# FFN in of a hybrid decoder block: splits one piece earlier, a weight sum moved from an adding DMA to VectorE, first sums by DMA, the second norm in a written order

## The chip, the cores and the metric

The kernel runs on 1 core of one Trainium2 chip. The metric is the device time of one launch, in microseconds; the profile adds the span of one profiled execution on that core. PE is TensorE, DVE VectorE, ACT ScalarE, POOL GpSimd and SP SyncE, which only issues DMAs here.

## What is computed

One layer, 512 tokens by 1024 features, all in float32:

```
mod = silu(c) @ mod_w + mod_b                 # shift1 scale1 gate1 shift2 scale2 gate2
h = rms_norm(x, g_pre_mix) * (1 + scale1) + shift1
...                                           # three mixers on h @ w_in, merged
mix_out = merged @ w_o
x = x + gate1 * rms_norm(mix_out, g_post_mix)
h2 = rms_norm(x, g_pre_ffn) * (1 + scale2) + shift2
gt, up = split(h2 @ w_ffn_in, 2)              # 1024 x 5632
f = (silu(gt) * up) @ w_ffn_out               # 2816 x 1024
x = x + gate2 * rms_norm(f, g_post_ffn)
```

The change lies between `mix_out` and `f`.

## The kernel before

**Products in three parts.** Every float32 operand of a matmul is split in two (`split`, L154 and L155): ACT casts it to a rounded copy (`whi`), DVE takes the difference to it (`wlo`). A product is then three matmuls (`mm3`): hi by hi, hi by lo, lo by hi. A weight piece is 128x1024; ACT's cast and DVE's difference of a later piece are issued when an earlier one is used: `piece()` splits up to `LOOK` = 3 pieces, the current one among them. Four buffers each hold `whi` and `wlo`.

**FFN in by seven products.** The 22 column blocks of 128 in each of gate and up are taken as 11 units of two (`u` = 0 to 10). A unit's 2x2 block product (two halves of the features by two column blocks, for two halves of the tokens) is done with seven products in place of eight. Its weights arrive as two raw tiles, `un[0]` and `un[1]`, each with two halves of the features. Four of the seven pieces are halves as loaded: q1, q2 from `un[0]`, q4 and q7 from `un[1]`, where q7's half has `un[0]`'s first half added to it. The other three are made in one tile, `wsum`, by running sums: q5 is the sum of the two halves of `un[1]` (DVE, L266); an adding DMA from POOL's queue (L274) then adds a half of `un[0]` for q6, and a second one the other half for q3. The half for q7 is added by another DMA of POOL (L267). A DMA of this kind reads its destination, adds, and writes. The second adding DMA of a unit can go only after q6's `wlo`, which reads the tile.

**A unit's steps.** From unit 2 on the pieces are used in the order 5, 1, 4, 6, 7, 2, 3; each is a `step` (L1135) of 24 matmuls of 256 columns. q5, q4, q7 and q1 each have a bank of PSUM of their own. After step 7, `gated_m1` builds two of the four output blocks `c` with three DVE operations (L1159, L1160, L1162) and takes their sigmoid on ACT (`sigm`, L164 to L166, three activations); its products on DVE (L1144, L1145) are held back until after the next piece's split (`flush`). Step 2 adds into q1's bank and gives a third block (`gated_m0`); step 3 adds into q5's bank, once c has read it, and `third_of` (L1167) gives the fourth. Units 0 and 1 are run together, product by product, since the token halves become ready late.

**What sets the order.** In FFN in, PE, DVE and ACT run in the order in which the code is written (`manual_schedule`). Each engine takes its own queue in order, and an instruction whose input isn't there holds up all behind it. SP loads raw tiles when their buffers come free, about a unit ahead.

**The second norm.** Between `w_o` and FFN in, each block of 128 tokens goes through `x1_chain`: squares of the two PSUM halves (ACT, L1048), `rstd_from` (Ln and Exp on ACT, L150, L151), the scaled product by `G1` (DVE, L1055), the add into `x1` (L1057), squares of that, its product by the second scale on POOL (`xm`, L1060), a second `rstd_from`, and the last scale and shift on DVE (L1065). `h2_tr` (L1074) transposes the result; `t1r` to `t4r` are the sums of token halves that the seven products need, each two DVE operations from `hbh` and `hbl` and a split.

**FFN out.** Its first operand, `fparts`, is the split of a finished unit; unit 0's is made in the last unit, ahead of step 3, the others one after another as the products need them.

Of the kernel before, what the change touches and what calls it, by code (L numbers as in the profile page):

```python
# [7 lines left out]
F32 = mybir.dt.float32  # L8
# [5 lines left out]
P = 128  # L14
# [18 lines left out]
def hybrid_block(ctx: ExitStack, tc, x, c, mod_w, mod_b, g_pre_mix, g_post_mix, g_pre_ffn,  # L33
# [35 lines left out]
    def q2(name, dt=F32):  # L69
        return tq.tile([P, 512], dt, tag="q2", name=name, bufs=12)  # L70
# [3 lines left out]
    def t2(name, dt=F32):  # L74
        return tp.tile([P, 512], dt, tag="t2", name=name, bufs=NT2)
# [92 lines left out]


    chunks, pieces, raws = [], [], []  # L170
    at = {"dma": 0, "split": 0, "use": 0, "raw": 0}

    def w_cols(src, c0, n=256):

# [69 lines left out]
    def wino_load(u, i):  # L244
# [6 lines left out]
        for g in range(2):  # L251
# [3 lines left out]
        units[u][i] = [raw[:, :, 4 * a:4 * a + 4].rearrange("p g k n -> p g (k n)")  # L255
                       for a in range(2)]

    def wino_piece(u, q):
        if u not in units:
            units[u] = {}  # L260
            for i in range(1 if u == 1 else 2):
                wino_load(u, i)
        un = units[u]
        if q == 5:
            un["s"] = late_pool["fx"].tile([P, 2, 512], F32, tag="wsum", name="wsum", bufs=2)
            vec.tensor_tensor(un["s"], un[1][0], un[1][1], ALU.add)  # L266
            nc.gpsimd.dma_start(un[1][0], un[0][0], accum_op=ALU.add)  # L267
        src = {1: (0, 0), 2: (0, 1), 4: (1, 1), 7: (1, 0)}.get(q)
        src = un[src[0]][src[1]] if src else un["s"]
        hi = wp.tile([P, 1024], FR, tag="whi", name="whi").rearrange("p (g n) -> p g n", g=2)  # L270
        lo = wp.tile([P, 1024], FR, tag="wlo", name="wlo").rearrange("p (g n) -> p g n", g=2)
        split(hi, lo, src)
        if q in (5, 6):
            nc.gpsimd.dma_start(un["s"], un[0][q - 5], accum_op=ALU.add)  # L274
        return [t_.rearrange("p g (k n) -> p g k n", k=4) for t_ in (hi, lo)]
# [768 lines left out]
    def x1_chain(tb, pos):  # L1044
        st = sm.tile([P, 6], F32, tag="st", name="st", bufs=4)
        for hf in range(2):
            sq = t2("sq2")
            act.activation(sq, pos[hf], AF.Square, accum_out=st[:, hf:hf + 1])  # L1048
        vec.tensor_tensor(st[:, 0:1], st[:, 0:1], st[:, 1:2], ALU.add)
        rstd_from(st[:, 2:3], st[:, 0:1], D)  # L1050
        xms = []
        for hf in range(2):
            t_ = t2("t2k")
            xv = x1[:, tb, half(hf)]
            vec.scalar_tensor_tensor(t_, pos[hf], st[:, 2:3], G1[hf], op0=ALU.mult,  # L1055
                                     op1=ALU.mult)
            vec.tensor_tensor(xv, xv, t_, ALU.add)  # L1057
            act.activation(t_, xv, AF.Square, accum_out=st[:, 3 + hf:4 + hf])
            xm = q2("xm")
            pool.tensor_tensor(xm, xv, SC[hf], ALU.mult)  # L1060
            xms.append(xm)
        vec.tensor_tensor(st[:, 3:4], st[:, 3:4], st[:, 4:5], ALU.add)
        rstd_from(st[:, 5:6], st[:, 3:4], D)
        for hf in range(2):
            vec.scalar_tensor_tensor(xms[hf], xms[hf], st[:, 5:6], SH[hf], op0=ALU.mult,  # L1065
                                     op1=ALU.add)
        return xms

    def h2_tr(tb, xms):
        pts = []  # L1070
        for q in range(2):
            pt = bank("pt2")
            for j in range(4):
                pe.transpose(pt[:, blk(j)], xms[q][:, blk(j)], ident)  # L1074
            pts.append(pt.rearrange("p (k t) -> p k t", k=4))
        return pts

    def h2_tiles(tb, xms):

        for q, p3 in enumerate(h2_tr(tb, xms)):  # L1080
            split(hbh[:, q, :, blk(tb)], hbl[:, q, :, blk(tb)], p3)

    todo = []
    for tp2 in range(2):
        tbs = (2 * tp2, 2 * tp2 + 1)
        pos = {tb: [bank("pwo") for _ in range(2)] for tb in tbs}
        ws = {}
        for k in range(KD - LATE):
            ws[k] = piece()
            for tb in tbs:  # L1090
                wo_mm(pos[tb], tb, ws[k], k)
            if todo and k >= 2:
                h2_tiles(*todo.pop(0))
        for k in range(KD - LATE, KD):
            ws[k] = piece()
        for tb in tbs:
            for k in range(KD - LATE, KD):
                wo_mm(pos[tb], tb, ws[k], k)
            todo.append((tb, x1_chain(tb, pos[tb])))


    ma.close()
    fp = ctx.enter_context(tc.tile_pool(name="fp", bufs=1, reuse_waits="tile"))
    fxs = ExitStack()
    fx = fxs.enter_context(tc.tile_pool(name="fx", bufs=1, reuse_waits="tile"))
    late_pool.update(fp=fp, fx=fx)
    wino_load(1, 1)

    def f4_tile(name, dt=F32):
        return fp.tile([P, 2, T], dt, tag="f4", name=name, bufs=NU)  # L1110
# [61 lines left out]
        fhs.append(parts_[0])  # L1172
        fls.append(parts_[1])
    f4s, fhs, fls, pts = [], [], [], {}
    with tc.manual_schedule(engines={ET.PE, ET.DVE, ET.Activation}):
# [6 lines left out]
        for u in range(2):  # L1182
            fresh(1)
            act.copy(u2s[u], pb_[1][u])
        for u in range(2):
            step(2, pb_[1][u], False, True)
            pts[u] = h2_tr(*todo.pop(0))

        t1_, b22, t2_, t3_, t4_ = (f4_tile(n) for n in ("t1r", "b22", "t2r", "t3r", "t4r"))

        def k4(t_, u):
            return t_[:, u, :].rearrange("p (k t) -> p k t", k=4)

        def parts_of(q, t_, u):
# [4 lines left out]
        for q in (6, 7, 4):  # L1199
            tx[q] = [[q2("tx", FR).rearrange("p (k t) -> p k t", k=2) for _ in range(2)]  # L1200
                     for _ in range(2)]
        tks = [slice(u * P, (u + 1) * P) for u in range(2)]
        for u in range(2):
# [4 lines left out]
            act.copy(k4(b22, u), pts[u][1])  # L1208
        for u in range(2):
# [6 lines left out]
            flush()  # L1216
        fresh(5)
        fresh(5)
        for u in range(2):
            vec.tensor_tensor(k4(t3_, u), k4(b22, u), pts[u][0], ALU.subtract)  # L1220
            parts_of(7, t3_, u)
# [1 line left out]
            fresh(6)  # L1223
            vec.tensor_tensor(u2s[u], pb_[6][u], u2s[u], ALU.add)
        for u in range(2):
            vec.tensor_tensor(k4(t4_, u), hbh[:, 1, :, tks[u]].bitcast(F32), k4(t2_, u), ALU.add)
            vec.tensor_tensor(k4(t4_, u), k4(t4_, u), hbl[:, 1, :, tks[u]].bitcast(F32), ALU.add)
# [10 lines left out]
        for u in range(2, NU):  # L1238
            f4s.append(f4_tile("f4"))
            p5 = bank("pf5")  # L1240
            step(5, p5, True, True)
            p1, u2 = bank("pf1"), temp("u2", 512, 2)
            step(1, p1, True, True)
            act.copy(u2, p1)
            p4 = bank("pf4")
            step(4, p4, True, True)
            p6 = bank("pf6")
            step(6, p6, True, True)
            vec.tensor_tensor(u2, p6, u2, ALU.add)
# [10 lines left out]
        flush()  # L1260
    fxs.close()
    tqs.close()
    fo = ctx.enter_context(tc.tile_pool(name="fo", bufs=1, reuse_waits="tile"))
# [100 lines left out]
```

## Time and profile before

| | |
|---|---|
| median of 3 runs | 868.24 us (867.53 to 868.84) |
| profiled execution, its own time | 870.63 us |
| its span | 868.9 us |
| mean granted clock of PE | 0.975 |
| PE, DVE, ACT, POOL busy | 90%, 64%, 49%, 20% of the span |
| end of w_o, transition, units 2 to 10 of FFN in, FFN out | to 431.4, to 499.7, to 731.0, to 868.9 us |
| adding DMAs wsum<-wraw | 22 of 512 KB, median 6.0 us from issue to landing |
| adding DMAs wraw<-wraw | 11 of 512 KB, median 5.2 us |

A row of the page's groups names a line, an engine, an operation, and output<-input by the program's names, then how often, its busy time and the idle time ahead of it with what ended most of that. A row of the timeline has the start, the length and, in brackets, how long the engine stood idle and what released it. A row of the windows has from:to, the length, then busy time and count of PE, PE's weight loads, DVE, ACT and POOL, PE's clock, the share of the DMA engines and GB/s. A row of the waits has a total, how often, and the longest.

### The profile page before, as it was taken

The numbers are of one execution on the slowest core, as the hardware profiler recorded it, in microseconds if no ns is written. First come the engines' busy times: TensorE is split into PE (matmuls) and PEld (weight loads), VectorE is DVE, ScalarE is ACT, GpSimd is POOL, SyncE is SP. The second block draws the span as 40 slices with busy tenths as digits, with TensorE's granted clock in tenths as the row PEclk, the third lists the DMA queues.
The fourth block names the chain that finished last, engine by engine and source line by source line (L and its number), as shares of the span: only waits on it lengthen the run. The fifth ranks groups of instructions, "written<-read, shape, count | busy, mean of one in ns | idle before, by whom it ended". The sixth has DMA issues, their size and how long they took to land. (4 is left out here: it accounts for less than half of the span.)

```text
span 868.9 us, 11371 instructions
## 1 busy us (share of the span) xinstructions
PE 779.5 (90%) x4357; PEld 664.8 (77%) x4357; DVE 558.7 (64%) x801; ACT 421.6 (49%) x703; POOL 173.0 (20%) x208
## 2 busy tenths in 40 slices
PE   4899999999999999999859688788888888899997
PEld 3679887776788888878758677788788787678886
DVE  5999876678475665367777657556565676853223
ACT  5557544766673645336535444544445455523112
POOL 4344323355211110122241011111111110000000
PEclk9999999999999999999988999999999999999999
DMA  9963422114257867375356556687676647351302
GB/s 281 296 202 97 129 68 95 49 57 153 82 185 211 264 188 233 108 221 201 109 108 131 150 106 137 147 170 158 139 153 132 125 105 228 106 212 62 114 1 97
DMA packets 122390, 126.14 MB, mean 145 GB/s; under 512 B 4124, under 2 KB 93264, under 8 KB 122336
## 3 DMA queue, kind: packets, MB, share of 16 engines
q1 hardware_dynamic: 109008, 99.62, 37.3%
q0 software_dynamic: 12560, 24.73, 16.0%
q10 hardware_dynamic: 768, 1.07, 0.3%
q8 instruction: 34, 0.56, 0.3%
q14 instruction: 20, 0.16, 0.1%
HBM read 102.33 MB, written 2.10 MB: 120 GB/s over the span
## 5 line engine op out<-in xcount | busy, mean ns | idle before, releaser
L155 DVE TENSOR_TENSOR wlo<-wraw,whi 128x1024 fp32r<-128x1024 f32 (+1 forms) x133 | 164.1, 1243 | 106.3 <-ACT whi L154 106.2
L154 ACT CAST whi<-wraw 128x1024 fp32r<-128x1024 f32 (+1 forms) x133 | 135.5, 1032 | 123.1 <-PE pgt L159 33.6
L1135 PE MATMUL pf<-hbh,whi 128*128 128x256 f32 x352 | 102.9, 292 | 28.7 <-DVE c L1160 11.8
L1135 PE MATMUL pf<-tx,whi 128*128 128x256 f32 x528 | 101.0, 293 | 8.9 <-ACT whi L154 8.9
L1135 PE MATMUL pf<-hbh,wlo 128*128 128x256 f32 x352 | 101.7, 289 | 7.4 <-DVE wlo L155 7.4
L1135 PE MATMUL pf<-hbl,whi 128*128 128x256 f32 x352 | 100.9, 287 | 0.1
L1135 PEld LDWEIGHTS pf<-hbh,whi 128*128 128x128 f32 x352 | 68.6, 195 | 32.6 <-issue 13.3
L1135 PEld LDWEIGHTS pf<-tx,whi 128*128 128x128 f32 x528 | 84.8, 197 | 10.8 <-ACT whi L154 10.7
L1135 PE MATMUL pf<-tx,wlo 128*128 128x256 f32 x264 | 77.6, 294 | 8.0 <-DVE wlo L155 7.9
L1135 PEld LDWEIGHTS pf<-hbh,wlo 128*128 128x128 f32 x352 | 68.8, 195 | 9.5 <-DVE wlo L155 9.5
L158 PE MATMUL pgt<-hh,whi 128*128 128x512 f32 x192 | 75.6, 394 | 0.0
L160 PE MATMUL pgt<-hh,wlo 128*128 128x512 f32 x192 | 75.4, 393 | 0.0
L159 PE MATMUL pgt<-hl,whi 128*128 128x512 f32 x192 | 75.0, 391 | 0.0
L155 DVE TENSOR_TENSOR wlo<-wsum,whi 128x1024 fp32r<-128x1024 f32 x33 | 40.3, 1223 | 50.3 <-ACT whi L154 50.2
L1135 PEld LDWEIGHTS pf<-hbl,whi 128*128 128x128 f32 x352 | 68.9, 196 | 0.5 <-DVE hbl L155 0.4
L158 PE MATMUL pfo<-whi,fparts 128*128 128x512 f32 x154 | 62.3, 405 | 5.5 <-ACT fparts L154 5.5
L154 ACT CAST whi<-wsum 128x1024 fp32r<-128x1024 f32 x33 | 34.2, 1040 | 66.7 <-DMA wsum<-wraw 61.0
L160 PE MATMUL pfo<-whi,fparts 128*128 128x512 f32 x154 | 61.9, 406 | 0.3 <-DVE fparts L155 0.3
L159 PE MATMUL pfo<-wlo,fparts 128*128 128x512 f32 x154 | 61.8, 401 | 0.0
L1135 PEld LDWEIGHTS pf<-tx,wlo 128*128 128x128 f32 x264 | 52.3, 198 | 10.5 <-DVE wlo L155 10.5
L274 POOL DMA_DIRECT2D wsum<-wraw x22 | 26.4, 1204 | 109.2 <-DVE wlo L155 109.2
L974 DVE SCALAR_TENSOR_TENSOR macc<-wraw,sc,macc 128x512 f32<-128x512 f32 x56 | 42.6, 761 | 7.7 <-ACT macc L972 4.7
(385 smaller groups left out, 1709.7 us busy)
## 6 DMA issues: line engine op xcount, KB each, us to landing
wraw<-in_w_ffn_in_dram SPq DMA_DIRECT2D x44, 512.0 KB, 6.7
wraw<-in_w_in_dram SPq DMA_DIRECT2D x20, 1024.0 KB, 5.2
wraw<-in_mod_w_dram SPq DMA_DIRECT2D x16, 1024.0 KB, 5.9
wsum<-wraw POOLq DMA_DIRECT2D x22, 512.0 KB, 6.0
wraw<-in_w_ffn_out_dram SPq DMA_DIRECT2D x10, 1024.0 KB, 5.0
wraw<-in_mod_w_dram SPq DMA_DIRECT2D x16, 512.0 KB, 6.8
wraw<-in_w_o_dram SPq DMA_DIRECT2D x8, 1024.0 KB, 5.2
wraw<-wraw POOLq DMA_DIRECT2D x11, 512.0 KB, 5.2
```

The lines of the kernel that those rows point to most:

```text
L154: act.copy(hi, src)
L155: vec.tensor_tensor(lo, src, hi.bitcast(F32), ALU.subtract)
L158: pe.matmul(o, whi, xhi, start=start, stop=False)
L159: pe.matmul(o, whi, xlo, start=False, stop=False)
L160: pe.matmul(o, wlo, xhi, start=False, stop=stop)
L274: nc.gpsimd.dma_start(un["s"], un[0][q - 5], accum_op=ALU.add)
L974: vec.scalar_tensor_tensor(acc, mw[:, r], c_, acc, op0=ALU.mult, op1=ALU.add)
L1135: pe.matmul(o[:, cs], a_[:, g, k, :], b_, start=(start and g + k + part == 0), stop=(stop and k == 3 and part == 2), skip_group_check=True)
```

## The change

- From the second half of `w_o` on, `piece()` splits up to 4 pieces, not 3 (for one step of the transition again 3).
- For units 2 to 10 the half for q7 is added on DVE (L284), when q4 is split, in place of POOL's DMA.
- For units 0 and 1, q5's sum is made by DMA: SP loads half of `un[1]` a second time straight into `wsum` (four loads of 256 KB, L267), and POOL's adding DMAs add the other half (L271). Their q7 halves stay with POOL's DMA (L272).
- `x1_chain` becomes five functions. The product by `G1` is made in PSUM beside the rstd; one DVE operation then scales and adds into `x1`; `xm` is made on DVE, not POOL. For blocks 2 and 3 the functions are called in a written order with the last matmuls of `w_o`, inside the manual schedule.
- ACT copies the transposes as they are (`braw`, 4 of them), and `t1r` and `t4r` take one DVE operation each from the copy in place of two.
- `fparts` of unit 0 is made after the last unit's step 5.

```diff
-        while at["split"] < min(i + LOOK, n_pieces):
+        while at["split"] < min(i + at["look"], n_pieces):
...
+    def wino_open():
+
+        for u in range(2):
+            units[u]["s"] = wsum_tile()
+            for g in range(2):
+                c0 = g * FFN + (2 * u + 1) * P
+                nc.sync.dma_start(units[u]["s"][:, g].rearrange("p (k n) -> p k n", k=4),
+                                  w_ffn_in[0:512, c0:c0 + P].rearrange("(k p) n -> p k n", k=4))
+            if u:
+                wino_load(1, 1)
+            nc.gpsimd.dma_start(units[u]["s"], units[u][1][1], accum_op=ALU.add)
+            nc.gpsimd.dma_start(units[u][1][0], units[u][0][0], accum_op=ALU.add)
...
-        if q == 5:
-            un["s"] = late_pool["fx"].tile([P, 2, 512], F32, tag="wsum", name="wsum", bufs=2)
+        if q == 5 and u > 1:
+            un["s"] = wsum_tile()
             vec.tensor_tensor(un["s"], un[1][0], un[1][1], ALU.add)
-            nc.gpsimd.dma_start(un[1][0], un[0][0], accum_op=ALU.add)
+        if q == 4 and u > 1:
+            vec.tensor_tensor(un[1][0], un[1][0], un[0][0], ALU.add)
...
+    def chain_norm(tb, pos):
+
+        st = sts[tb]
         vec.tensor_tensor(st[:, 0:1], st[:, 0:1], st[:, 1:2], ALU.add)
         rstd_from(st[:, 2:3], st[:, 0:1], D)
         for hf in range(2):
+            vec.tensor_tensor(pos[hf], pos[hf], G1[hf], ALU.mult)
+
+    def chain_x1(tb, pos, junk):
+        st, xms[tb] = sts[tb], []
+        xvs = [x1[:, tb, half(hf)] for hf in range(2)]
+        for hf, xv in enumerate(xvs):
+            vec.scalar_tensor_tensor(xv, pos[hf], st[:, 2:3], xv, op0=ALU.mult, op1=ALU.add)
+            act.activation(junk(), xv, AF.Square, accum_out=st[:, 3 + hf:4 + hf])
+        for hf, xv in enumerate(xvs):
+            xms[tb].append(q2("xm"))
+            vec.tensor_tensor(xms[tb][hf], xv, SC[hf], ALU.mult)
...
+            raws2[q, tb] = q2("braw").rearrange("p (k t) -> p k t", k=4)
+            act.copy(raws2[q, tb], p3)
...
+        if tp2:
+            at["look"] = 4
...
+        late_mm(2)
+        chain_sq(2, pos[2])
+        chain_norm(2, pos[2])
+        late_mm(3)
+        chain_x1(2, pos[2], lambda: t2("sq2"))
+        chain_sq(3, pos[3])
+        chain_norm2(2)
+        chain_norm(3, pos[3])
+        chain_h2(2)
...
+        wino_open()
...
-            vec.tensor_tensor(k4(t1_, u), hbh[:, 0, :, tks[u]].bitcast(F32), pts[u][0],
-                              ALU.subtract)
-            vec.tensor_tensor(k4(t1_, u), k4(t1_, u), hbl[:, 0, :, tks[u]].bitcast(F32), ALU.add)
+            vec.tensor_tensor(k4(t1_, u), raws2[0, u], pts[u][0], ALU.subtract)
...
             step(5, p5, True, True)
+            if u == NU - 1:
+                t_ = fp.tile([P, 2, 2, T], FR, tag="raw4", name="fparts", bufs=1)
+                f_parts(0, (t_[:, 0], t_[:, 1]))
...
-            if u == NU - 1:
-                t_ = fp.tile([P, 2, 2, T], FR, tag="raw4", name="fparts", bufs=1)
-                f_parts(0, (t_[:, 0], t_[:, 1]))
```

How this moves the queues shows best in the order of the instructions. DVE in one of the units 2 to 10, before, from the splits of q7 and q2 (`wlo<-wraw x2`) to the fourth block's `u`; the first `wlo<-wsum` is q3's, the second the next unit's q5:

```order
L155 TENSOR_TENSOR wlo<-wraw,whi 128x1024 x2
L1249 TENSOR_TENSOR u_4861<-pf_4921,u_4861 128x512
L155 TENSOR_TENSOR wlo<-wsum,whi 128x1024
L1159 TENSOR_TENSOR c_4980<-pf_4951,u_4861 128x512
L1160 SCALAR_TENSOR_TENSOR c_4980<-pf_4829,c_4980 128x512
L1162 TENSOR_TENSOR c_4980<-pf_4892,c_4980 128x512
L266 TENSOR_TENSOR wsum<-wraw 128x1024
L155 TENSOR_TENSOR wlo<-wsum,whi 128x1024
```

And now the same stretch:

```order
L155 TENSOR_TENSOR wlo<-wraw,whi 128x1024 x2
L155 TENSOR_TENSOR wlo<-wsum,whi 128x1024
L1316 TENSOR_TENSOR u_4874<-pf_4933,u_4874 128x512
L282 TENSOR_TENSOR wsum<-wraw 128x1024
L155 TENSOR_TENSOR wlo<-wsum,whi 128x1024
L1195 TENSOR_TENSOR c_5001<-pf_4963,u_4874 128x512
L1196 SCALAR_TENSOR_TENSOR c_5001<-pf_4841,c_5001 128x512
L1198 TENSOR_TENSOR c_5001<-pf_4904,c_5001 128x512
```

The sum and the split for the next unit's q5 have moved from behind the three operations of c to ahead of them, and the add into `u` from ahead of q3's split to behind it.

DVE further on in the same unit, before; `wlo<-wraw` is here q1's and then q4's of the next unit, the last row q6's, and `f<-sg,u` begins the products of the fourth block:

```order
L1145 TENSOR_TENSOR f_4828<-f_4828,c_4980 128x512
L155 TENSOR_TENSOR wlo<-wraw,whi 128x1024
L1144 TENSOR_TENSOR f_4828<-sg_5028,pf_4860 128x256
L1145 TENSOR_TENSOR f_4828<-f_4828,pf_4860 128x256
L1167 TENSOR_TENSOR u_4861<-pf_4829,u_4861 128x512
L155 TENSOR_TENSOR wlo<-wraw,whi 128x1024
L1144 TENSOR_TENSOR f_4828<-sg_5063,u_4861 128x256
L1145 TENSOR_TENSOR f_4828<-f_4828,u_4861 128x256
L155 TENSOR_TENSOR wlo<-wsum,whi 128x1024
```

And now, from the end of c's products to the fourth block's:

```order
L1181 TENSOR_TENSOR f_4840<-f_4840,c_5001 128x512
L284 TENSOR_TENSOR wraw<-wraw 128x2x512
L155 TENSOR_TENSOR wlo<-wraw,whi 128x1024
L1180 TENSOR_TENSOR f_4840<-sg_5039,pf_4873 128x256
L1181 TENSOR_TENSOR f_4840<-f_4840,pf_4873 128x256
L1203 TENSOR_TENSOR u_4874<-pf_4841,u_4874 128x512
L155 TENSOR_TENSOR wlo<-wsum,whi 128x1024
L1180 TENSOR_TENSOR f_4840<-sg_5075,u_4874 128x256
L1181 TENSOR_TENSOR f_4840<-f_4840,u_4874 128x256
```

The new add stands ahead of q4's split; q6's split now follows the add into `u` directly, with q4's split and the fourth block's products no longer between.

ACT in the transition now: `st` and `sg_3833` belong to the norm of the last block, the two casts of `wsum` are q5's of units 0 and 1, and the copies of `u` are what PE's steps 2 of units 0 and 1 wait for:

```order
L154 CAST whi<-wraw 128x1024
L1236 COPY u_3800<-pf_3802 128x512
L1081 ACTIVATE sg_3833,st<-x_3361 128x512
L1081 ACTIVATE sg_3836,st<-x_3361 128x512
L154 CAST whi<-wsum 128x1024
L1239 COPY u_3801<-pf_3842 128x512
L150 ACTIVATE st<-st,eps_c 128x1
```

Before, both copies of `u` stood ahead of both casts; the first cast now stands ahead of the second copy.

More of the change, by code (lines that the diff above doesn't have):

```diff
@@ L170, in hybrid_block @@
     chunks, pieces, raws = [], [], []
-    at = {"dma": 0, "split": 0, "use": 0, "raw": 0}
+    at = {"dma": 0, "split": 0, "use": 0, "raw": 0, "look": LOOK}
     def w_cols(src, c0, n=256):
@@ L256, in wino_load, with wsum_tile @@
                        for a in range(2)]
+    def wsum_tile():
+        return late_pool["fx"].tile([P, 2, 512], F32, tag="wsum", name="wsum", bufs=2)
+    def wino_open():
[9 more added lines that the diff above has]
+            nc.gpsimd.dma_start(units[u][1][0], units[u][0][0], accum_op=ALU.add)
     def wino_piece(u, q):
@@ L1042, in wo_mm, with chain_sq, chain_norm2, chain_h2 @@
                 w[1][:, 0, half(hf)], k == 0, k == KD - 1)
[L1044 to L1045 removed]
+    sts, xms = {}, {}
+    def chain_sq(tb, pos):
+        st = sts[tb] = sm.tile([P, 6], F32, tag="st", name="st", bufs=4)
         for hf in range(2):
[L1047 to L1048 removed]
+            act.activation(t2("sq2"), pos[hf], AF.Square, accum_out=st[:, hf:hf + 1])
+    def chain_norm(tb, pos):
+        st = sts[tb]
         vec.tensor_tensor(st[:, 0:1], st[:, 0:1], st[:, 1:2], ALU.add)
         rstd_from(st[:, 2:3], st[:, 0:1], D)
[L1051 removed]
         for hf in range(2):
[L1053 to L1061, printed above, removed]
+            vec.tensor_tensor(pos[hf], pos[hf], G1[hf], ALU.mult)
[8 more added lines that the diff above has]
+            vec.tensor_tensor(xms[tb][hf], xv, SC[hf], ALU.mult)
+    def chain_norm2(tb):
+        st = sts[tb]
         vec.tensor_tensor(st[:, 3:4], st[:, 3:4], st[:, 4:5], ALU.add)
         rstd_from(st[:, 5:6], st[:, 3:4], D)
+    def chain_h2(tb):
         for hf in range(2):
[L1065 to L1069, printed above, removed]
+            vec.scalar_tensor_tensor(xms[tb][hf], xms[tb][hf], sts[tb][:, 5:6], SH[hf],
+                                     op0=ALU.mult, op1=ALU.add)
+    def h2_tr(tb):
         pts = []
@@ L1073, in h2_tr, with h2_tiles, late_mm @@
             for j in range(4):
-                pe.transpose(pt[:, blk(j)], xms[q][:, blk(j)], ident)
+                pe.transpose(pt[:, blk(j)], xms[tb][q][:, blk(j)], ident)
             pts.append(pt.rearrange("p (k t) -> p k t", k=4))
         return pts
-    def h2_tiles(tb, xms):
-        for q, p3 in enumerate(h2_tr(tb, xms)):
+    raws2 = {}
+    def h2_tiles(tb):
+        for q, p3 in enumerate(h2_tr(tb)):
             split(hbh[:, q, :, blk(tb)], hbl[:, q, :, blk(tb)], p3)
+            raws2[q, tb] = q2("braw").rearrange("p (k t) -> p k t", k=4)
+            act.copy(raws2[q, tb], p3)
+    def late_mm(tb):
+        for k in range(KD - LATE, KD):
+            wo_mm(pos[tb], tb, ws[k], k)
     todo = []
@@ L1092, in hybrid_block @@
             if todo and k >= 2:
-                h2_tiles(*todo.pop(0))
+                h2_tiles(todo.pop(0))
         for k in range(KD - LATE, KD):
             ws[k] = piece()
+        if tp2:
+            break
         for tb in tbs:
[L1097 to L1107, printed above, removed]
+            late_mm(tb)
+            chain_sq(tb, pos[tb])
+            chain_norm(tb, pos[tb])
+            chain_x1(tb, pos[tb], lambda: t2("sq2"))
+            chain_norm2(tb)
+            chain_h2(tb)
+            todo.append(tb)
     def f4_tile(name, dt=F32):
@@ L1174, in hybrid_block @@
     f4s, fhs, fls, pts = [], [], [], {}
-    with tc.manual_schedule(engines={ET.PE, ET.DVE, ET.Activation}):
+    rest = ctx.enter_context(ExitStack())
+    rest.enter_context(tc.manual_schedule(engines={ET.PE, ET.DVE, ET.Activation}))
+    if True:
+        late_mm(2)
[7 more added lines that the diff above has]
+        chain_h2(2)
+        ma.close()
+        fp = ctx.enter_context(tc.tile_pool(name="fp", bufs=1, reuse_waits="tile"))
+        fxs = ExitStack()
+        fx = fxs.enter_context(tc.tile_pool(name="fx", bufs=1, reuse_waits="tile"))
+        late_pool.update(fp=fp, fx=fx)
+        wino_open()
         pb_ = {1: [], 5: [], 6: [], 7: [], 4: []}
@@ L1181, in hybrid_block @@
         u2s = [temp("u2", 512, 2) for _ in range(2)]
[L1182 to L1187, printed above, removed]
+        fresh(1)
+        act.copy(u2s[0], pb_[1][0])
+        chain_x1(3, pos[3], lambda: temp("sg1", 512))
+        fresh(1)
+        act.copy(u2s[1], pb_[1][1])
+        chain_norm2(3)
+        step(2, pb_[1][0], False, True)
+        pts[0] = h2_tr(2)
         t1_, b22, t2_, t3_, t4_ = (f4_tile(n) for n in ("t1r", "b22", "t2r", "t3r", "t4r"))
@@ L1192, in k4, with tx_tiles @@
             return t_[:, u, :].rearrange("p (k t) -> p k t", k=4)
+        def tx_tiles(q):
+            tx[q] = [[q2("tx", FR).rearrange("p (k t) -> p k t", k=2) for _ in range(2)]
+                     for _ in range(2)]
         def parts_of(q, t_, u):
@@ L1198, in parts_of, with t1_of @@
                 split(h_, l_, k4(t_, u)[:, k0:k0 + 2, :])
-        for q in (6, 7, 4):
-            tx[q] = [[q2("tx", FR).rearrange("p (k t) -> p k t", k=2) for _ in range(2)]
-                     for _ in range(2)]
         tks = [slice(u * P, (u + 1) * P) for u in range(2)]
-        for u in range(2):
-            vec.tensor_tensor(k4(t1_, u), hbh[:, 0, :, tks[u]].bitcast(F32), pts[u][0],
-                              ALU.subtract)
-            vec.tensor_tensor(k4(t1_, u), k4(t1_, u), hbl[:, 0, :, tks[u]].bitcast(F32), ALU.add)
+        def t1_of(u):
+            vec.tensor_tensor(k4(t1_, u), raws2[0, u], pts[u][0], ALU.subtract)
             split(hbh[:, 3, :, tks[u]], hbl[:, 3, :, tks[u]], k4(t1_, u))
             act.copy(k4(b22, u), pts[u][1])
+        t1_of(0)
+        chain_h2(3)
+        at["look"] = 3
+        step(2, pb_[1][1], False, True)
+        at["look"] = 4
+        pts[1] = h2_tr(3)
+        t1_of(1)
+        tx_tiles(6)
         for u in range(2):
@@ L1225, in hybrid_block @@
         for u in range(2):
-            vec.tensor_tensor(k4(t4_, u), hbh[:, 1, :, tks[u]].bitcast(F32), k4(t2_, u), ALU.add)
-            vec.tensor_tensor(k4(t4_, u), k4(t4_, u), hbl[:, 1, :, tks[u]].bitcast(F32), ALU.add)
+            vec.tensor_tensor(k4(t4_, u), raws2[1, u], k4(t2_, u), ALU.add)
+        tx_tiles(4)
+        for u in range(2):
             parts_of(4, t4_, u)
@@ L1260, in hybrid_block @@
         flush()
+    at["look"] = LOOK
     fxs.close()
```

1 line of the change is left out of this document (added).

## The prediction

> **What bounds the kernel now.** I read the page first, for the busiest engine and the chain that ended last.
>
> ```profile
> span 868.9 us, 11371 instructions
> PE 779.5 (90%) x4357; PEld 664.8 (77%) x4357; DVE 558.7 (64%) x801; ACT 421.6 (49%) x703; POOL 173.0 (20%) x208
> ...
> DMA wsum<-wraw 9%; PE pfo L159 3%; PE pfo L160 3%; PE pfo L158 3%; DVE wlo L155 3%; ACT whi L154 2%; PE pf L1135 2%; DMA wraw<-in_mod_w_dram 2%; DMA macc<-in_mod_b_dram 1%; DVE macc L974 1%; ACT sg L165 1%; DVE fparts L155 1%; DVE c L1159 1%; DVE c L1160 1%; ACT sg L164 1%
> ```
>
> PE is 90% busy, yet the chain's largest line is no matmul: it is the adding DMA wsum<-wraw. So I went to the stage of that line, units 2 to 10 of FFN in (first row of the windows, last PE busy time), and to PE's waits there.
>
> ```profile
> 499.70:731.00 231.30, 194.33 (x1512) 185.41 (x1512) 141.60 (x176) 107.60 (x158) 32.38 (x28) 0.98 0.67 142
> ```
> ```profile
> PE pf L1135 <- DVE wlo L155: 14.0, 19, 0.8
> PE pf L1135 <- ACT whi L154: 11.9, 17, 1.5
> PE pf L1135 <- DVE c L1160: 9.5, 8, 2.3
> ```
>
> Of 231.3 us PE is busy for 194.3 and waits for the other engines in each unit. Who sets the pace shows in one unit of the timeline, from c of one unit (573.32) to c of the next (598.09). Columns: start, length, engine.
>
> ```profile
> 573.32 0.68 DVE L1159 TENSOR_TENSOR c<-pf,u 128x512 f32<-128x512 f32 x1
> ...
> 575.37 1.22 DVE L266 TENSOR_TENSOR wsum<-wraw 128x1024 f32<-128x1024 f32 x1
> 578.51 1.22 DVE L155 TENSOR_TENSOR wlo<-wsum,whi 128x1024 fp32r<-128x1024 f32 x1 [1.92 <-ACT whi L154]
> 579.65 0.68 DVE L1144 TENSOR_TENSOR f<-sg,c 128x512 f32<-128x512 f32 x1
> ...
> 580.98 1.22 DVE L155 TENSOR_TENSOR wlo<-wraw,whi 128x1024 fp32r<-128x1024 f32 x1
> 582.12 0.41 DVE L1144 TENSOR_TENSOR f<-sg,pf 128x256 f32<-128x256 f32 x1
> ...
> 586.06 1.23 DVE L155 TENSOR_TENSOR wlo<-wraw,whi 128x1024 fp32r<-128x1024 f32 x1 [2.47 <-ACT whi L154]
> ...
> 588.00 1.22 DVE L155 TENSOR_TENSOR wlo<-wsum,whi 128x1024 fp32r<-128x1024 f32 x1
> ...
> 593.16 0.69 DVE L1249 TENSOR_TENSOR u<-pf,u 128x512 f32<-128x512 f32 x1 [1.68 <-PE pf L1135]
> 596.95 1.23 DVE L155 TENSOR_TENSOR wlo<-wsum,whi 128x1024 fp32r<-128x1024 f32 x1 [3.09 <-ACT whi L154]
> 598.09 0.69 DVE L1159 TENSOR_TENSOR c<-pf,u 128x512 f32<-128x512 f32 x1
> ```
> ```profile
> 577.45 1.03 ACT L154 CAST whi<-wsum 128x1024 fp32r<-128x1024 f32 x1
> ...
> 595.87 1.05 ACT L154 CAST whi<-wsum 128x1024 fp32r<-128x1024 f32 x1 [6.51 <-DMA wsum<-wraw]
> ```
> ```profile
> 576.89 1.20 POOL L267 DMA_DIRECT2D wraw<-wraw  x1 [10.91 <-DVE wsum L266]
> ...
> 589.51 1.20 POOL L274 DMA_DIRECT2D wsum<-wraw  x1 [8.28 <-DVE wlo L155]
> ```
>
> This is a closed loop. c releases the sigmoids on ACT; between and behind them stand, in queue order, the splits of q5, q1, q4 and q6 of the next unit; q6's wlo (588.00) releases the second adding DMA (589.51); the cast of q3 waits until it has landed (595.87); q3's wlo stands ahead of the next c. The period is 16.19 (c to the DMA's issue) + 6.36 (issue to cast) + 2.22 (cast to c) = 24.77 us. ACT, DVE and PE all idle within it: the loop is latency, and **what stands on it counts, not what an engine is busy with**.
>
> **The change, part by part.** *1. Splits one piece earlier (look 4).* The aim is that PE waits less for whi and wlo. In DVE's queue, however, the add of u (L1316), the sum for q5 (L282) and q5's wlo now stand between q3's wlo and c. All three are behind the landing, so they lengthen the loop there: u add about 0.60 (its slot, a little under 593.16's 0.69), the sum 1.22, 0.08 from it to the cast, cast to wlo 1.06 (578.51-577.45), wlo 1.14 (579.65-578.51). That is +4.1: cast to c becomes 6.3. Before, the sum lay beside ACT's sigmoids (575.37, with DVE idle for 1.92 behind it) and the u add ran while the DMA did, so both cost nothing; this cover is gone. In exchange q6's wlo no longer stands behind q4's wlo and the third products (586.06 to 588.00, 1.94): -1.94.
>
> *2. Sum for q7 on DVE (L284).* One 128x1024 add a unit, nearest row the 1.22 of 575.37, slot 1.14. It stands between the products of c and q4's wlo, ahead of u, sigmoid and q6's split, so it is on the loop: +1.14. With part 1, c to issue becomes 16.19+1.14-1.94 = 15.39. On the other side a third of the unit's adding DMAs goes.
>
> *3. How long the DMA then takes.* No row shows the new mix, so I bound it:
>
> ```profile
> 689.86 1.20 POOL L274 DMA_DIRECT2D wsum<-wraw  x1 [8.28 <-DVE wlo L155]
> ...
> 714.08 1.20 POOL L274 DMA_DIRECT2D wsum<-wraw  x1 [8.28 <-DVE wlo L155]
> ```
> ```profile
> 522.36 0.68 DVE L1159 TENSOR_TENSOR c<-pf,u 128x512 f32<-128x512 f32 x1
> ```
> ```profile
> 695.14 1.05 ACT L154 CAST whi<-wsum 128x1024 fp32r<-128x1024 f32 x1 [5.44 <-DMA wsum<-wraw]
> ...
> 721.30 1.05 ACT L154 CAST whi<-wsum 128x1024 fp32r<-128x1024 f32 x1 [7.38 <-DMA wsum<-wraw]
> ```
>
> Without weight loads behind it, issue to cast is 5.28 (689.86 to 695.14); the last takes 7.22. From c of unit 2 (522.36) to the last cast (721.30) are 198.94 us: eight times 16.19, seven times 2.22 and eight DMAs leave 53.9/8 = 6.7 for one. The loads that share its time wait for q7's wlo; the third products now stand ahead of that, which puts them about 0.8 later behind the DMA, so I take 6.2; ends 5.28 and 6.7.
>
> Sum for the stage: 8x15.39 + 7x6.34 + 8x6.2 = 217.1 against 198.9: **+18.2 us** (ends +10.8 and +22).
>
> By the Trainium skill ("DMA: Bandwidth & Descriptors", "Anatomy of one DMA — SWDGE (gpsimd) path") such a DMA takes about 2.0 us plus its bytes at 436 KB a microsecond, an estimate of 3.2 us for 512 KB. By it the stage would lose nothing; the undisturbed 5.28 above speaks against it for an adding transfer, and I go by the row.
>
> *4. Second norm, first sums, t1 and t4.*
>
> ```profile
> 418.17 0.66 PE L1074 MATMUL pt<-ident,xm 128*128 128x128 f32 x4 [2.50 <-DVE xm L1065]
> ...
> 420.40 0.63 PE L160 MATMUL pwo<-whi,ml 128*128 128x512 f32 x1
> 420.82 0.63 PE L158 MATMUL pwo<-whi,mh 128*128 128x512 f32 x1
> ...
> 424.17 0.39 PE L160 MATMUL pwo<-whi,ml 128*128 128x512 f32 x1
> 424.40 0.39 PE L158 MATMUL pwo<-whi,mh 128*128 128x512 f32 x1
> ...
> 441.97 0.58 PE L1135 MATMUL pf<-hbh,whi 128*128 128x256 f32 x1 [4.75 <-ACT u L1184]
> ...
> 457.35 0.58 PE L1135 MATMUL pf<-hbh,whi 128*128 128x256 f32 x1 [5.72 <-ACT hbh L154]
> ```
> ```profile
> 440.16 2.89 POOL L1060 TENSOR_TENSOR xm<-x,SHSC 128x512 f32<-128x512 f32 x2 [4.14 <-DVE x L1057]
> ```
>
> The eight POOL products (1.4 us each in the row) go to DVE and one of two DVE operations of each half goes, so the wait of 2.50 at 418.17 should go, and with it some 8 matmuls at 0.42 apart in place of 0.23: 4.1. Of the waits of 4.75 and 5.72 little can go: the first sums now come as loads and then adding DMAs, the first not before the squares of the last block, that is two transfers of 5 us or so in a row behind the end of w_o, and ACT's cast of it stands ahead of the copy of u2 that PE's next step needs. On the other side two DVE sums of 1.22 and four DVE operations leave the way of t1 and t4. I take **-6** in all; ends 0 and -14.6 (all three waits and the slow matmuls gone). If the second sum lands 3 us late, this falls to -3.
>
> *5. First fparts ahead.*
>
> ```profile
> 732.00 0.50 PE L158 MATMUL pfo<-whi,fparts 128*128 128x512 f32 x1 [3.32 <-ACT fparts L154]
> ...
> 741.60 0.50 PE L158 MATMUL pfo<-whi,fparts 128*128 128x512 f32 x1 [2.19 <-ACT fparts L154]
> ```
>
> The wait of 3.32 goes, since unit 0's parts then stand ready; the 2.19 at 741.60 hangs on the last unit's chain and stays. **-3.3**, ends 0 and -5.5. It also ends the stage: what follows is PE alone.
>
> Total: 18.2 - 6 - 3.3 = +8.9. The profiled run took 870.63 (its span and 1.7 around it) and so becomes 879.5; it lies 2.4 above the median of 868.24, from which **877.1** follows.
>
> **The rivals.** *A, the DMA gets free (not slower).* With one adding DMA of three gone and the loads later, each could take 5.28 as the undisturbed row: +10.8-9.3 = +1.5, 869.7; with the transition at -10 it is 866. It turns at about 5.1 us of the DMA. Against it: the DMA that goes was issued at 576.89, 12.6 us ahead of the one that counts (589.51), so it was hardly what lengthened that. *B, the look-ahead does what it says:* PE finds each piece ready, and the 14.0+11.9 us of waits for wlo and whi go; 868.24-25.9-9.3 = 833. Against it: c still stands behind the landing, and step q3 adds into the bank that c's second operation (L1160 before) must have read. *C, the DMA stays at 6.7 and the first sums are late:* +22-3-3.3, 884. *D, the clock:* PE now stands for some 5 us before q3 in each unit. After the 2.50 at 418.17 matmuls came 0.42 apart in place of 0.23; a step of 24 (2.85) would lose about 2.3, and were it on the loop, 8 more such give +18 and 895. Against it: the step has some 3 us before u needs it. The Trainium skill ("TensorE: Matmul & The Clock Gate", "What's actually happening") halves the clock after an idle window of about 3.4 us; the trace shows it after 2.50 already, so by both the step is slow, and both leave the time as it is.
>
> **How the numbers follow.** Forecast 0.70 (871 to 882); A 0.12, B 0.05, C 0.09, D 0.04. Range 867 to 884: it leaves out B, D and the ends of A and C. 0.2% (1.7 us) is about what a measurement tells from no change. Faster: B and half of A's, 0.10; same: the rest of A, 0.07; slower 0.83.
>
> **What would show it.** Right: c to c near 28 us in units 3 to 9, q5's wlo directly ahead of c on DVE, PE waiting 5 us for c before q3, the adding DMA still the largest line of the chain; pfo starting without the 3.3. Wrong: a period under 25, or issue to cast at 5.3 throughout, or a wait for wsum in units 0 and 1 that outlasts what part 4 gains.

## The result, and the profile after

The changed kernel takes 882.01 us (median of 4 runs, 881.74 to 882.73); the kernel before takes 868.54 (4 runs, 867.53 to 869.38). The ratio is 1.0157, 95% interval 1.0139 to 1.0174: slower by 13.5 us, where 8.9 were forecast.

The page of the kernel after, its span, engines and chain:

```profile
span 880.0 us, 11357 instructions
PE 778.7 (88%) x4357; PEld 670.8 (76%) x4357; DVE 561.9 (64%) x812; ACT 423.1 (48%) x707; POOL 149.5 (17%) x193
...
DMA wsum<-wraw 8%; PE pfo L160 3%; PE pfo L159 3%; PE pfo L158 3%; ACT whi L154 2%; DVE wlo L155 2%; DVE macc L991 1%; PE pf L1171 1%; DMA macc<-in_mod_b_dram 1%; DVE wsum L282 1%; DVE u L1316 1%; DMA wraw<-in_mod_w_dram 1%; ACT sg L165 0%; DVE fparts L155 0%; ACT sg L164 0%
```

The engines' work is nearly the same: VectorE has 3.2 us more, ScalarE 1.5 more, PE 0.8 less. The chain still runs through wsum<-wraw, and the sum for q5 (L282) and the add into u (L1316) have joined it. PE's waits in the window of the units before (499.7 to 731; the changed kernel's units run on to 741, with one more wait of 2.3 us for c):

```profile
PE pf L1171 <- DVE c L1196: 46.1, 8, 6.5
PE pf L1171 <- DVE wlo L155: 2.4, 5, 0.8
PE pf L1171 <- ACT whi L154: 1.0, 1, 1.0
```

The look-ahead did what it was meant to: the waits for wlo and whi fell from 14.0 and 11.9 us to 2.4 and 1.0. But the wait for c, 9.5 before, is now 46.1, more than the two gave. One unit of the timeline of DVE, of ACT and of POOL shows why:

```profile
572.76 0.68 DVE L1195 TENSOR_TENSOR c<-pf,u 128x512 f32<-128x512 f32 x1
...
580.41 1.22 DVE L284 TENSOR_TENSOR wraw<-wraw 128x1024 f32<-128x1024 f32 x1
...
586.63 1.23 DVE L155 TENSOR_TENSOR wlo<-wsum,whi 128x1024 fp32r<-128x1024 f32 x1 [2.48 <-ACT whi L154]
...
595.50 1.23 DVE L155 TENSOR_TENSOR wlo<-wsum,whi 128x1024 fp32r<-128x1024 f32 x1 [4.58 <-ACT whi L154]
596.64 0.68 DVE L1316 TENSOR_TENSOR u<-pf,u 128x512 f32<-128x512 f32 x1
597.25 1.22 DVE L282 TENSOR_TENSOR wsum<-wraw 128x1024 f32<-128x1024 f32 x1
599.65 1.23 DVE L155 TENSOR_TENSOR wlo<-wsum,whi 128x1024 fp32r<-128x1024 f32 x1 [1.19 <-ACT whi L154]
600.79 0.68 DVE L1195 TENSOR_TENSOR c<-pf,u 128x512 f32<-128x512 f32 x1
```
```profile
594.42 1.05 ACT L154 CAST whi<-wsum 128x1024 fp32r<-128x1024 f32 x1 [5.44 <-DMA wsum<-wraw]
598.57 1.04 ACT L154 CAST whi<-wsum 128x1024 fp32r<-128x1024 f32 x1 [3.10 <-DVE wsum L282]
```
```profile
588.15 1.18 POOL L291 DMA_DIRECT2D wsum<-wraw  x1 [13.83 <-DVE wlo L155]
```

From c (572.76) to the second adding DMA's issue (588.15) are 15.39 us, to the cast 6.27 more (594.42), to the next c 6.37 (600.79): 28.03 in place of 24.77. The rows from 595.50 to 600.79 are the price: q3's split, then u, the sum, ScalarE's cast of it and q5's wlo, one after another behind the landing, and only then c.

| stretch, us | before | after | difference | forecast |
|---|---|---|---|---|
| start to c of unit 2 | 522.36 | 516.14 | -6.2 | -6 |
| c of unit 2 to the last cast of wsum | 198.94 | 216.88 | +17.9 | +18.2 |
| that cast to the end of the span | 147.60 | 146.98 | -0.6 | -3.3 |

### The profile page after: what moved, and what is told of

Its sections match the earlier page's. It is cut to its first block, busy times and chain, and to the rows that moved or that the text cites. A ratio compares the mean times of both kernels' runs of the same rounds, so it can differ in the third digit from the quotient of the medians.

```text
span 880.0 us, 11357 instructions
## 1 busy us (share of the span) xinstructions
PE 778.7 (88%) x4357; PEld 670.8 (76%) x4357; DVE 561.9 (64%) x812; ACT 423.1 (48%) x707; POOL 149.5 (17%) x193
## 5 line engine op out<-in xcount | busy, mean ns | idle before, releaser
L1171 PE MATMUL pf<-hbh,whi 128*128 128x256 f32 x352 | 109.8, 312 | 62.5 <-DVE c L1196 53.2
L1171 PEld LDWEIGHTS pf<-hbh,whi 128*128 128x128 f32 x352 | 76.0, 216 | 65.3 <-issue 55.3
L1171 PE MATMUL pf<-hbl,whi 128*128 128x256 f32 x352 | 107.5, 305 | 0.1
L1171 PE MATMUL pf<-hbh,wlo 128*128 128x256 f32 x352 | 106.9, 304 | 0.0
L1171 PE MATMUL pf<-tx,whi 128*128 128x256 f32 x528 | 95.5, 282 | 2.0 <-ACT whi L154 1.0
L1171 PEld LDWEIGHTS pf<-tx,whi 128*128 128x128 f32 x528 | 81.1, 188 | 2.6 <-ACT whi L154 1.2
L1171 PE MATMUL pf<-tx,wlo 128*128 128x256 f32 x264 | 75.3, 285 | 2.8 <-DVE wlo L155 2.7
L1171 PEld LDWEIGHTS pf<-hbl,whi 128*128 128x128 f32 x352 | 76.1, 216 | 0.5 <-DVE hbl L155 0.4
L1171 PEld LDWEIGHTS pf<-hbh,wlo 128*128 128x128 f32 x352 | 75.5, 215 | 0.0
L1171 PEld LDWEIGHTS pf<-tx,wlo 128*128 128x128 f32 x264 | 49.7, 188 | 4.5 <-DVE wlo L155 4.4
```

The source lines that it names most:

```text
L1171: pe.matmul(o[:, cs], a_[:, g, k, :], b_, start=(start and g + k + part == 0), stop=(stop and k == 3 and part == 2), skip_group_check=True)
```

## The experiments

Theory 1 is the prediction's: **the loop through the second adding DMA sets units 2 to 10, and the order of the queues behind its landing decides.** Its rivals: the add that came to VectorE costs; PE's slowed clock costs; and, for what was missing in the tail, the place of the gate's products.

**Look 3 again in the units.**

```diff
+        at["look"] = 3
         for u in range(2, NU):
```

> The changed kernel with the look-ahead back at 3 pieces from unit 2 on; all else stays. Theory 1 (the loop through the second adding DMA sets units 2 to 10, and look 4 lengthened it): c to the DMA's issue 16.2 us (the add for q7 falls into DVE's idle time ahead of q4's wlo, 2.47 before), issue to cast 6.3, cast to c 2.2, so c to c 24.7 in place of 28.0; c of unit 2 to the last cast of wsum some 195 in place of 216.9, and the time about 860. Rival 2 (the add for q7 on VectorE is what costs, and the look-ahead is harmless): c to c stays near 27 to 28, time within 3 us of 882. Rival 3 (PE's slowed clock is what costs): PE's waits of 5 us for c go here too, so only the c-to-issue part tells it from 1: under 3 it shortens by the slow step's 2.3.

862.73 us (ten runs, 856.76 to 869.82), ratio to before 0.9921 (0.9886 to 0.9956). One unit of POOL, DVE and ACT, c of unit 4 to c of unit 5:

```profile
580.95 1.18 POOL L291 DMA_DIRECT2D wsum<-wraw  x1 [8.30 <-DVE wlo L155]
```
```profile
564.75 0.68 DVE L1195 TENSOR_TENSOR c<-pf,u 128x512 f32<-128x512 f32 x1
...
574.94 1.22 DVE L284 TENSOR_TENSOR wraw<-wraw 128x1024 f32<-128x1024 f32 x1
577.49 1.23 DVE L155 TENSOR_TENSOR wlo<-wraw,whi 128x1024 fp32r<-128x1024 f32 x1 [1.34 <-ACT whi L154]
...
589.55 0.68 DVE L1195 TENSOR_TENSOR c<-pf,u 128x512 f32<-128x512 f32 x1
```
```profile
587.33 1.05 ACT L154 CAST whi<-wsum 128x1024 fp32r<-128x1024 f32 x1 [5.76 <-DMA wsum<-wraw]
```

16.20 + 6.38 + 2.22 = 24.80 us, and 198.05 from c of unit 2 to the last cast. The same add on VectorE (574.94) costs nothing here: it lies in the idle time ahead of q4's wlo, which was 2.47 and is 1.34. Rival 2 is out, and so is rival 3, by its own measure: c to issue is longer than after the change (15.39), not shorter. With the look-ahead back at 3 in the units the kernel is 19 us faster, and the rest of the change is a gain. The stage is 3 us longer than expected: issue to cast is 6.5 in the mean, not 6.3, and the last unit, in which fparts now stands in VectorE's queue, takes 17.3 from c to issue.

**Look 3, and q7's sum by DMA again.**

```diff
+        at["look"] = 3
         for u in range(2, NU):
...
-        if q == 4 and u > 1:
-            vec.tensor_tensor(un[1][0], un[1][0], un[0][0], ALU.add)
...
             vec.tensor_tensor(un["s"], un[1][0], un[1][1], ALU.add)
+            nc.gpsimd.dma_start(un[1][0], un[0][0], accum_op=ALU.add)
```

> Look 3 from unit 2 on, and the sum for q7 by an adding DMA of GpSimd's queue again (units 2 to 10): what is left of the change are the transition and the tail. Theory 1: c to c as before the change, 24.8 (16.2 + 6.4 + 2.2); issue to cast longer than in look3 if the third adding DMA or the earlier loads lengthen it (6.7 against 6.3 in the mean), so c of unit 2 to the last cast 198, time 862 to 864. Rival 2: 7 or more us below look3, since the add left VectorE.

861.31 us, ratio to before 0.9925 (0.9900 to 0.9951); not to be told from look3, and a little under the expected 862 to 864; the stage takes 199.5, not 198. Issue to landing of the second adding DMA is about 6.3 in half of the units, as in look3, but 7.4 and 7.3 in two of eight, where look3 has 7.1 once (and both some 7.1 in the last unit). That the third adding DMA lengthens the second one now and then is not shown by this: in the unit with 7.3 here, the kernel before, which has the third one too, took 7.5 in its first profile and 6.2 in its second.

**Look 4, and q7's sum by DMA again.** The second and third piece of the last diff, without the first.

> Look 4 stays, the sum for q7 goes back to an adding DMA. Theory 1: the add stood on the loop, 1.14 us a unit: c to issue 14.25 in place of 15.39, cast to c stays 6.35; issue to cast 6.3 to 6.7. c of unit 2 to the last cast 209 to 212, time 874 to 877. Rival 2: c to issue shortens by more than 2 and the time returns to 868 or less.

874.65 us, ratio 1.0067 (1.0044 to 1.0090). The stage, 207.6, is shorter than the expected 209 to 212, since issue to cast is 6.1 in the mean, not 6.3 to 6.7. From the timelines of DVE and POOL:

```profile
570.45 0.68 DVE L1194 TENSOR_TENSOR c<-pf,u 128x512 f32<-128x512 f32 x1
...
597.35 0.68 DVE L1194 TENSOR_TENSOR c<-pf,u 128x512 f32<-128x512 f32 x1
```
```profile
584.70 1.18 POOL L290 DMA_DIRECT2D wsum<-wraw  x1 [12.08 <-DVE wlo L155]
```

c to issue is 14.25, 1.14 less than after the change, to the hundredth the slot of one add; c to c 26.9. Rival 2 is out. With look 4 the add stands on the loop, with look 3 it does not: **the same operation costs 1.1 us or nothing, by where it stands in its queue.** Taken off in this order, some 9 us of the stage's loss are the add (216.9 to 207.6), and the other 8 are look 4 by itself (207.6 against look3_q7dma's 199.5).

**First sums on VectorE again.**

```diff
     def wino_open():
-
-        for u in range(2):
...
+        wino_load(1, 1)
...
-        if q == 5 and u > 1:
+        if q == 5:
...
+            if u < 2:
+                nc.gpsimd.dma_start(un[1][0], un[0][0], accum_op=ALU.add)
```

> The changed kernel with the first sums of units 0 and 1 made on VectorE from the loaded tiles, as before the change. Theory 1 (the first sum by DMA is late, and ScalarE's cast of it holds up the copy of u that PE waits 7.5 us for): that wait falls to 3 or less, c of unit 2 comes 2 to 5 us earlier than 516.1 (over 1.5 us of DVE work back), the rest is the same: time 877 to 880. Rival (the DMA sums took work from VectorE's way and gained): c of unit 2 1 to 3 us later, 883 to 885.

878.47 us, ratio to before 1.0122 (1.0078 to 1.0166). PE's longest wait in the transition, first of the kernel after, then of this one:

```profile
PE pf L1171 <- ACT u L1239: 7.5, 1, 7.5
```
```profile
PE pf L1163 <- ACT u L1231: 2.8, 1, 2.8
```

c of unit 2 comes at 513.2 in place of 516.1, and the median is 3.5 lower, though the two ratios' intervals overlap. The trace is clearer: from the end of `w_o` to c of unit 2 are 87.0 us here, and 91.7 to 92.1 after the change and in three other kernels with the first sums by DMA and look 4 (q7dma, rest, restclose). The first sums by DMA cost: ScalarE's cast of the late sum holds up the copy behind it.

**The written order closed behind FFN in.** The change opens the written order of PE, VectorE and ScalarE for FFN in and never closes it, so it holds through FFN out, too.

```diff
     at["look"] = LOOK
+    rest.close()
     fxs.close()
```

> The changed kernel with the written order of PE, VectorE and ScalarE ending with FFN in, as before the change, so that the gate's products (macc) are placed by the scheduler again. Theory 1 for the tail: the changed kernel's new wait of 2.1 us of PE for mah comes from the macc operations standing later in VectorE's queue; here PE waits under 0.5 for mah, and second pfo to end is 127.3 as before in place of 130.3; some macc stand between the operations of c again, which takes back up to 2. Time 879 to 881.5. Rival: the loss behind the second pfo comes from the late end of FFN in itself; then nothing moves, 882.

884.83 us, ratio 1.0205 (1.0177 to 1.0234), against the expectation. The mechanism was half right. PE's waits behind 731 us, first of the kernel after, then of this one:

```profile
PE pfo L158 <- ACT fparts L154: 2.5, 1, 2.5
PE pf L1171 <- DVE c L1196: 2.3, 1, 2.3
PE pmr L968 <- ACT mah L154: 2.1, 1, 2.1
```
```profile
PE pfo L158 <- ACT fparts L154: 9.0, 1, 9.0
PE pfo L160 <- DVE fparts L155: 1.4, 1, 1.4
```

The wait for mah is gone, as expected, but the scheduler's order lets PE wait 9.0 us for fparts; last cast to end is 151.6 in this profile, whose run lay 4 us above the kernel's median.

**The gate's row products one piece later.** With `rest` true, the generator gives up its turn once more between the gate's split and PE's row products:

```diff
-                sides.append(mods_in_turn([(5, hf) for hf in range(2)], False, mah_late))
+                sides.append(mods_in_turn([(5, hf) for hf in range(2)], True, mah_late))
```

> The changed kernel with only the gate's row products on PE one weight piece later in FFN out. Theory 1 for the tail (PE's stand at pmr for mah gives back what the earlier first fparts gained): that wait of 2.1 us goes, last cast of wsum to end 144.5 in place of 147.0, time 879 to 880. Rival: the operations that follow wait instead, time 882.

879.09 us, ratio to before 1.0103 (1.0049 to 1.0156). The interval overlaps that of the change, but the tail tells them apart: no wait for mah is left, and last cast to end is 142.73 in place of 146.98 (147.1 to 148.6 in four other kernels with the row products where the change has them). So 4.2 us of the tail hung on that wait and what stood behind it, more than the 2.5 expected; the wait itself is 2.1 of them, and where the rest lies isn't shown.

**The kernel before, profiled again.**

> The kernel before, profiled a second time, for the 2.1 us by which its first profiled run lay above the median. If the extra time came from the adding DMAs, the two units with issue to cast of 7.6 to 7.8 us (the others 6.3) differ from run to run, and c of unit 2 to the last cast is 197 to 198 in place of 198.9; if it came from the transition or the tail, that sum is 198.9 again and c of unit 2 or last cast to end is shorter.

Span 868.1 us. c of unit 2 comes at 521.35, the stage takes 197.94, the tail 148.8: each lies 1 us or so off the first profile, in both directions. What the first expectation named came (the stage is in 197 to 198, and of the two long DMAs one is short here), but c of unit 2 is earlier and the tail longer, too. The extra 2 us of one run are spread, and their cause stays open. So a part that is read from one profile of each kernel is good to 1 us or so, and to 3 where it starts at the span's start (c of unit 2 comes at 516.1 after the change and at 519.4 in restclose).

**Another order of the splits (swap3).** If the loop is the cause, an order that takes work off it must beat both kernels. A list of its own now says in which order pieces are split; they are used as before. `ahead` splits up to the piece that it names.

```diff
+    USED = WINO + [(u, q) for u in range(2, NU) for q in (5, 1, 4, 6, 7, 2, 3)]
+    WINO += [(2, 5)]
+    for u in range(2, NU):
+        WINO += [(u, q) for q in (1, 6, 4, 7, 2)]
+        WINO += [(u + 1, 5)] if u + 1 < NU else []
+        WINO += [(u, 3)]
...
             step(5, p5, True, True)
+            ahead(u, 4)
+            if third:
+                third_of(*third)
...
+            ahead(u, 7)
             step(1, p1, True, True)
...
+            ahead(u, 2)
             step(4, p4, True, True)
...
+            ahead(u, 3)
             step(7, p7, True, True)
             gated_m1(f4s[u], p4, p5, p7, u2)
+            if u < NU - 1:
+                ahead(u + 1, 1)
...
+            if u < NU - 1:
+                ahead(u + 1, 6)
             step(3, p5, False, True)
-            third_of(f4s[u], p5, u2)
+            third = (f4s[u], p5, u2)
```

> Another order of the splits in units 2 to 10 (q5 of the next unit ahead of q3, then q1, q6, q4, q7, q2; the next unit's q6 split ahead of the fourth block's sigmoid, which moves behind the next step 5), with all else of the change. It takes q5's sum and split, q4's split and the third sigmoid off the loop: c to the second adding DMA's issue about 9 to 10 us, and landing to c no more on the path. Theory 1: the loop falls under PE's own 20 us a unit (7 steps of 2.85), c to c 20.5 to 22, PE waits under 1 us a step; time 822 to 835. Rival (the waits only move, since DVE with 17 us and ACT with 13 us of work a unit can't keep up with PE in this order): c to c 24 or more, 850 and above.

850.71 us, ratio to before 0.9795 (0.9778 to 0.9812). c to issue is 9.2, as expected, but c to c 23.35, not 20.5 to 22: the DMA lands long before it is needed, and PE waits twice 1.5 us a unit, for q4's wlo behind the add for q7, and for c behind the sum for q5. The time is outside theory 1's range and on the rival's side (850 and above), the period between the two: the loop was not the only limit, VectorE's queue is the next.

**swap3 with the gate's row products later.** Both edits above.

> swap3 with the row products of the gate (PE's pmr, which waits for mah) one weight piece later in FFN out, 24 matmuls or 5.6 us. Theory 1 for the tail: PE's wait for mah (2 to 4 us in the changed kernel and in look3) goes, the rest is the same; 2 to 4 us under swap3. Rival: the products are then waited for by what reads the gate at the end of the first half, and nothing is gained.

843.61 us, ratio 0.9722 (0.9699 to 0.9746): 7 us under swap3, in place of 2 to 4; last cast to end falls from 150.8 to 142.15. PE's waits for mah in swap3 were 5.2 us, more than the 2 to 4 assumed.

**The two sums moved in VectorE's queue (swap4).** On top of both edits above:

```diff
-        if q == 4 and u > 1:
+        if q == 7 and u > 1:
             vec.tensor_tensor(un[1][0], un[1][0], un[0][0], ALU.add)
...
             ahead(u, 2)
+            if u < NU - 1:
+                wino_sum(u + 1)
```

`wino_sum` makes the sum for q5 of the next unit; the first sums are on VectorE, as in the run above.

> swap3_rest with the sum for q5 made before the add into u (in the time in which VectorE waits for step 6), the sum for q7 made when q7 is split (behind the fourth block's u, so that q4's wlo comes 1.1 us earlier), and the first sums on VectorE. Theory 1: of PE's two waits of 1.5 us a unit (for q4's wlo, for c) the first goes and the second falls to 0.5 or less; c to c 20.5 to 21.2 in place of 23.35, c of unit 2 3 us earlier; time 819 to 826. Rival: VectorE's queue stays the bound, c to c over 22.5, 835 or more.

828.30 us, ratio to before 0.9527 (0.9472 to 0.9583). The units' stage in the windows (from:to, length, PE's busy time first), first before the change, then after it, then here:

```profile
522.40:723.50 201.10, 170.69 (x1341) 163.18 (x1340) 123.52 (x153) 94.56 (x137) 28.82 (x24) 0.98 0.68 143
```
```profile
516.10:737.00 220.90, 176.62 (x1344) 174.12 (x1344) 132.50 (x162) 95.45 (x137) 18.86 (x16) 0.89 0.51 108
```
```profile
511.80:685.50 173.70, 163.42 (x1351) 160.33 (x1350) 130.72 (x160) 94.12 (x136) 18.13 (x16) 1.00 0.59 134
```

c to c is 21.6, a little over the 20.5 to 21.2 expected, PE is busy for 94% of the stage, and its clock is 1.00. VectorE has as much work as after the change (130.7 against 132.5), in an order in which PE waits for it for 9.4 us of the stage, after the change 47.7. PE's waits in the stage here:

```profile
PE pf L1181 <- DVE c L1206: 6.2, 7, 1.0
PE pf L1181 <- DVE wlo L155: 3.2, 8, 0.8
```

So the two waits of a unit shrank from 1.5 us each to 0.9 for c, where 0.5 or less was expected, and to 0.4 for wlo, which was to go. The time misses the expected 819 to 826 by 2.

## Why the prediction was right, point by point

- **What bounds:** right. The loop's three parts, taken from the rows before, give the unit shown after the change to within a tenth: 15.39, 6.27 and 6.37 against 15.39, 6.2 and 6.34. look3, look3_q7dma and q7dma move each part as its working says.
- **Part 1, look 4:** right. The u add, the sum and q5's split went behind the landing, +4.1 us a unit; the cover that had hidden them (ScalarE's sigmoids, the DMA's own time) was gone.
- **Part 2, q7's sum on VectorE:** right at +1.14 a unit with look 4; q7dma takes it away to the hundredth. That it costs nothing with look 3 was not said.
- **Part 3, the DMA's time:** right in size. In the mean it is (216.88 - 8x15.39 - 7x6.37)/8 = 6.15 us, 6.2 forecast. That the loads come later behind the DMA fits: with look 4 no second adding DMA of a unit took over 6.8 us from issue to landing, in five kernels, while with look 3 two or three of eight took 7.1 to 7.9 in each profile. Whether a third adding DMA in the unit lengthens the second, which rival A's objection held for unlikely, stays open (look3_q7dma). The Trainium skill's fit ("DMA: Bandwidth & Descriptors", "Anatomy of one DMA — SWDGE (gpsimd) path"), 3.2 us for this size, is not met by any run: the shortest adding DMAs of 512 KB took 5.0 us.
- **Part 4, the transition:** right in sign, -6.2 against -6, and the late first sum held up the copy of u as said; opensum shows it was worth 3 to 5 us. That the size fits to 0.2 is luck: c of unit 2 comes at 518.1 in rest and 519.4 in restclose, whose source is the same up to there, and at 521.4 in the second profile of before, so the gain lies between 2 and 6. It came ahead of the end of `w_o`, at 424.4 in place of 431.4, where the 2.50 and the slow matmuls are gone as told; from there to c of unit 2 nothing was gained (91.7 against 91.0). There the 5.72 shrank to 0.46 (before step 5), and the 4.75 grew to 7.53.
- **Part 5, the tail, is the term that was mis-sized:** -0.6 in place of -3.3 (the second profile of before would make it -1.8). Its own step held: from the last cast to the second wait for fparts are 16.7 us (733.02 to 749.73), 20.3 before. But 3.0 us came back behind it, where nothing was priced: with the written order open to the end the gate's sums stand later in VectorE's queue, and PE waits 2.1 us for mah, 0.3 before; restclose, which closes the order, has no such wait. rest takes that wait away and 4.2 us with it, all of them behind the second wait for fparts.
- **Rivals:** A had the DMA at 5.3, it took 6.15 in the mean; C had it at 6.7 and the gain of part 4 halved; in the number, 882.0 lies nearer to C's 884 than to 877.1, and the DMA's time is what speaks against it, since a gain of 3 in part 4 is not ruled out. B's own sentence came true, PE finds whi and wlo ready, and the time went to c, by the objection given there. D: the step behind the wait for c is slow, and the time does not hang on it, as said: the fourth block's u, which needs that step, starts without idle time behind the products ahead of it in VectorE's queue (583.47 in the unit shown). The first three matmuls of it:

```profile
602.35 0.55 PE L1171 MATMUL pf<-hbh,whi 128*128 128x256 f32 x1 [5.35 <-DVE c L1196]
602.69 0.42 PE L1171 MATMUL pf<-hbl,whi 128*128 128x256 f32 x1
602.91 0.42 PE L1171 MATMUL pf<-hbh,wlo 128*128 128x256 f32 x1
```

- **The total:** the spans differ by 11.1 (880.0 - 868.9), where the parts added up to 8.9: the tail gave 2.7 less than forecast, the other two parts together 0.5 more. The remaining 2.4 of the 13.5 lie in the single runs: the profiled run of before lay 2.1 above its median, the run after 0.3 below its own (881.74 against 882.01). The forecast took 2.4 off as if both stood alike.

## What to carry to other kernels

A split or sum that is issued earlier is earlier for one engine and stands ahead of something else on another: before a look-ahead is raised, ask what is queued behind the new rows on the in-order engine and whether a transfer's landing stands ahead of them. In a loop of latencies the same 1.1 us operation costs its full time or nothing, by its place; list the loop's parts from one unit of the timeline, and count an edit by what it moves on that list. When an edit opens a written order, see where it closes, and price what comes behind it too.

## What the runs showed of the hardware

The queues repeat closely: c to issue was 15.39 to 15.43 us in all eight units after the change. PE's matmuls stood 0.21 us apart behind a wait of 5.35 us, where 0.12 (a step of 24 in 2.85) is usual, and in the stage where it waited so once a unit its mean clock was 0.89 (0.98 before, 1.00 in swap4). Behind shorter waits it went both ways: the matmuls stood 0.21 us apart behind 2.84 us in opensum, and 0.12 behind 2.85 us in swap4. An adding DMA of 512 KB took 5.0 us when no load ran beside it and 6.2 in most units with weight loads behind it. With look 3 the second one of a unit took over 7 in two or three of eight units, with look 4 in none.
